# Two small norm tiles in another pool of a two-block fp32 network: the activation pool 160 bytes further on

## The chip, the cores and the metric

One core of a Trainium2 chip runs the whole program. The metric is the device time of one execution in microseconds, as the median of the runs. TensorE multiplies, with a stationary operand (128 x 128, brought in by its own instruction, the weight load) and a moving operand of up to 512 columns; VectorE (DVE), ScalarE (ACT) and GpSimd (POOL) do the rest, and SyncE (SP) issues most DMAs. SBUF, the working memory, has 128 partitions, and a tile takes the same bytes of each; an address below is a byte within a partition.

## What is computed

Two transformer blocks over 512 tokens of width 1024, in fp32. The first block has a mixer (sparse attention beside a matrix memory), a cross attention on a memory of 256 tokens and a feed-forward network; the second has four feed-forward networks, a convolution module and stick-breaking attention. What matters here is that nearly all of the work is matrix products, and that each stage starts with a norm over the features:

```python
def rms_norm(x, gain):
    xf = x.astype(jnp.float32)
    y = xf * lax.rsqrt(jnp.mean(xf * xf, axis=-1, keepdims=True) + NORM_EPS)
    return (y * gain.astype(jnp.float32)).astype(x.dtype)
...
def swiglu_ffn(h, w_gate_up, w_down):
    g, u = jnp.split(h @ w_gate_up, 2, axis=-1)
    return (jax.nn.silu(g) * u) @ w_down
...
def first_block(x, mem, ...):
        h = rms_norm(x, mix_norm_pre[l])
        y = hybrid_mixer(h, ...)
        x = x + rms_norm(y, mix_norm_post[l])
...
        h = rms_norm(x, ffn_norm_pre[l])
        y = swiglu_ffn(h, w_gate_up[l], w_down[l])
        x = x + rms_norm(y, ffn_norm_post[l])
```

## The kernel before

Activations lie feature-major: eight tiles of 128 features x 512 tokens. To keep fp32 accuracy, every operand is split into a rounded part (`hi`, or an `h` at the end of the name) and the remainder (`lo`, or `l`), and a product is three matmuls (`mm3`, lines 169 to 172): weights-hi by x-hi (L170), weights-hi by x-lo (L171), weights-lo by x-hi (L172). In a projection (`proj`, `projs`) the weights are the stationary operand, 128 columns of a slab `whi` or `wlo` at a time, and the activations are the moving operand, 512 columns, or 256 where a stage starts or ends with half of the tokens. In the products that give values token-major (`token_tiles`, L599 on) it is the other way round: 128 columns of `xh` are stationary and 256 columns of weights move. Rows name the output's PSUM tag, then the moving and the stationary operand: `sc<-xh,wlo`.

A feed-forward network (`ffn`) runs two halves. Each half projects 11 feature tiles, gate and up, from `xh` and `xl` (2 x 8 x 3 = 48 matmuls a tile, 528 a half), and multiplies the result, split into `hh` and `hl`, by the down weights (8 x 11 x 3 = 264 matmuls). There are five networks, so ten such halves; in two of the networks the first two feature tiles are projected in halves of the tokens (192 matmuls' worth in all). Other projections from `xh`/`xl` with 512 columns: 17 tiles of the mixer, 5 of the cross attention's queries, 14 of the convolution module, 8 keys and 8 queries of the stick-breaking attention, 24 matmuls each. The convolution module's second projection reads `ch`/`cl`, and half of the mixer's output product reads `yh`/`yl`; all these tiles share the buffers of `xh`/`xl`.

Weights come by DMA from SP's queue into `wraw` (three buffers), and are split by ACT (L126) and DVE (L130) into `whi` and `wlo` (four buffers each). The order of each engine's work is set by a scheduler that goes by data dependencies and a timeline of its own, in some places by hand (`order_pe`, `tick`).

Memory: pools are laid out one behind the other in the order in which they are opened, each tile padded to 32 bytes: `const` (vectors of gains, identity, ones), `act_p` (all activations that live long: `x`, `xh`, `xl`, squares, `rb`, and the small tiles `ms` and `rt` of the norm), `wp` (the weights), and behind these the pools of the stages. `ms` (two buffers of 16 bytes, the mean of squares) and `rt` (three buffers, its inverse root) are written in `rms_sums` (L247 on). From the built program:

| tiles | pool | address of the first | modulo 512 |
|---|---|---|---|
| xh, xl, and ch, cl, yh, yl in their place | act_p | 36,416 | 64 |
| whi, wlo | wp | 93,920 and 110,304 | 224 |
| hh, hl (feed-forward networks) | their own | 134,880 | 224 |
| ynh, ynl (mixer), oh, ol (cross attention) | yn, xp | 126,688 | 224 |
| pTh, and vh, its stationary operand | qp | 204,768 and 200,672 | 480 both |

All of these tiles follow one another at multiples of 1024 bytes, and weights are read in slices of 512 bytes, so that each tile or slice of a row of the table has the same address modulo 512.

Of the kernel before, what the change touches and what calls it, by code (L numbers as in the profile page):

```python
# [9 lines left out]
F32 = mybir.dt.float32  # L10
# [4 lines left out]
P = 128  # L15
S = 512
# [7 lines left out]
NEG = -1.0e30  # L24
# [24 lines left out]
def kernel(ctx: ExitStack, tc: tile.TileContext, t: dict, out: bass.AP):  # L49
# [85 lines left out]
    # heads of 64: the exact product of queries and keys in two passes, (q_hi + q_lo) (k_hi + k_lo), with the  # L135
    # parts of the keys on the two halves of the partitions and each part of the queries on both
# [16 lines left out]
    def head_scores(ps, q, k, i):  # L153
        """scores of query tile i with its keys, the first 128 (i + 1)"""
        n = max((i + 1) * P, 256)
        for c in range(2):
            nc.tensor.matmul(ps[:, :n], q[c][:, i * P : (i + 1) * P], k[:, :n], start=c == 0, stop=c == 1)

    def load_w(ap, width, raw=None, pieces=1, hp=1):
        """a slab of weights as its rounded part and the remainder"""  # L160
        if raw is None:
            raw = wp.tile([P, width], F32, tag="wraw", bufs=3, name=nm("wraw"))
            nc.sync.dma_start(raw, ap)
        hi = wp.tile([P, width], F32R, tag="whi", bufs=4, name=nm("whi"))
        lo = wp.tile([P, width], F32R, tag="wlo", bufs=4, name=nm("wlo"))
        split(raw, hi, lo, pieces=pieces, hp=hp)
        return hi, lo
# [6 lines left out]
    # steps of a latency chain, put between the products of a run that TensorE takes in program order  # L174
# [27 lines left out]
    def square_acc(src, j, state, ts=WHOLE, apart=False, eng=nc.gpsimd):  # L202
        """adds a tile's squares to the running sum; the last tile's may stay apart"""
        if j == KT - 1 and apart:
            if "last" not in state:
                state["last"] = act_p.tile([P, S], F32, tag="sqlast", name=nm("sqlast"))
            nc.scalar.activation(state["last"][:, ts], src[:, ts], AF.Square)
            return
        sq = act_p.tile([P, S], F32, tag="sq", bufs=2, name=nm("sq"))
        nc.scalar.activation(sq[:, ts], src[:, ts], AF.Square)  # L210
        if j == 0:
            state["first"] = sq
        elif j == 1:
            state["acc"] = act_p.tile([P, S], F32, tag="sqacc", name=nm("sqacc"))
            eng.tensor_tensor(state["acc"][:, ts], state["first"][:, ts], sq[:, ts], ALU.add)  # L215
        else:
            eng.tensor_tensor(state["acc"][:, ts], state["acc"][:, ts], sq[:, ts], ALU.add)

    def inv_rms(state, eps=1e-6, ts=WHOLE, psum_only=False):
        """(mean of squares + eps)^-1/2 per token: as a column per token tile, and as a row on all partitions"""  # L220
        if not state:
            for j in range(KT):
                square_acc(x[j], j, state, eng=nc.vector)
        sums = rms_sums(state, eps, ts)
        rt, pb = rms_rows(sums, ts)
        if psum_only:
            return rt, pb
        rb = act_p.tile([P, S], F32, tag="rb", bufs=2, name=nm("rb"))[:, : ts.stop - ts.start]
        nc.vector.tensor_copy(rb, pb)
        return rt, rb  # L230

    def inv_rms_chain(state, first, second):
        """the steps of inv_rms, after that many products each; the result is there when they are done"""
        if not state:
            for j in range(KT):
                square_acc(x[j], j, state, eng=nc.vector)
        got = []

        def finish():
            rt, pb = rms_rows(got[0], WHOLE)  # L240
            rb = act_p.tile([P, S], F32, tag="rb", bufs=2, name=nm("rb"))
            nc.vector.tensor_copy(rb, pb)
            got[:] = [rt, rb]

        chain.append([first, lambda: got.append(rms_sums(state, 1e-6, WHOLE))])
        chain.append([second, finish])
        return got  # L247

    def rms_sums(state, eps, ts):
        n = (ts.stop - ts.start) // P  # L250
        pr = at_tile()
        accs = [state[k] for k in ("acc", "last") if k in state]
        for a, acc in enumerate(accs):
            for i in range(n):
                c = ts.start + i * P
                nc.tensor.matmul(pr[:, 4 * a + i : 4 * a + i + 1], acc[:, c : c + P], ones[:, 0:1], start=True, stop=True)
        ms = act_p.tile([P, 4], F32, tag="ms", bufs=2, name=nm("ms"))
        nc.vector.tensor_scalar(ms[:, :n], pr[:, :n], 1.0 / D, eps, ALU.mult, ALU.add)
        if len(accs) == 2:
            nc.vector.scalar_tensor_tensor(ms[:, :n], pr[:, 4 : 4 + n], 1.0 / D, ms[:, :n], ALU.mult, ALU.add)  # L260
        rt = act_p.tile([P, 4], F32, tag="rt", bufs=3, name=nm("rt"))
        nc.gpsimd.tensor_tensor(rt[:, :n], ms[:, :n], nhalf[:, :n], ALU.pow)
        return rt
# [14 lines left out]
    def post_norm_add(y, state, nxt):  # L278
        """x += y * rb, where y carries its gain already; a step for each half of the tokens"""
# [23 lines left out]
    def ffn(fp, xs, st, wg, wu, wd, out_cb, head=0, tail=0, step=None):  # L303
        """head: F tiles whose projections start with the first half of the tokens; tail: output tiles that end so"""
# [91 lines left out]
    # =====================================================================  # L396
    # hybrid mixer
    # =====================================================================
# [32 lines left out]
    # relative bias: u[h, i] = bias_h(511 - i), masked distances NEG; T[q, c] = -u[127 - q + c]  # L431
# [32 lines left out]
    # gate rows: 0..23 branch gates, 32..35 input gate, 64..67 forget gate  # L464
# [23 lines left out]
    # compressed keys and values  # L488
# [61 lines left out]
    # cumulative gates of the matrix-memory heads  # L550
# [28 lines left out]
    # branch gates, token-major  # L579
# [6 lines left out]
    def token_tiles(chunks, wd, xs_, ntok, cb, ws=None):  # L586
        """out[tokens, wd] for each token tile; chunks hold 1024 / wd K tiles of wd columns"""
# [26 lines left out]
    def coef(sums, h, br, floor):  # L614
        """gate over the sum of the exponentials, per token"""
# [7 lines left out]
    def softmax_rows(ps, bias, ptile, sm, masked):  # L623
        """ps holds the negated scores; writes exp(score - max) to ptile and its row sums to sm"""
# [165 lines left out]
    for hp in range(2):  # L790
# [19 lines left out]
        for i in range(NT):  # L810
# [12 lines left out]
            # num / d, normalized: num * (mean(num^2) + eps d^2)^-1/2 with d = max(|den|, exp(-m))  # L823
# [64 lines left out]
    # =====================================================================  # L888
    # memory cross attention
    # =====================================================================  # L890
# [87 lines left out]
    # P: projection of a feature tile, Q: its query, S, V: a head's scores and values  # L978
# [21 lines left out]
    # =====================================================================  # L1000
    # feed-forward of the first block
    # =====================================================================
# [18 lines left out]
    # =====================================================================  # L1021
    # second block
    # =====================================================================
# [26 lines left out]
    # Depthwise taps on TensorE: 32 channels x 4 taps fill the rows, a diagonal per tap the columns,  # L1050
    # and four such column tiles run side by side; the other taps run on VectorE.
# [45 lines left out]
    def depthwise(j, sets, gl, R, wbd, ts=WHOLE):  # L1097
# [6 lines left out]
        # two independent chains of multiply-adds on VectorE  # L1104
# [17 lines left out]
    def ln_sums(ts):  # L1122
        """mean and variance per token"""
# [31 lines left out]
    def ln_finish(n, lm, m2, ts):  # L1155
        """SiLU of the normalized tiles"""
# [108 lines left out]
    def stick_scores(q, k):  # L1265
        Ws = []
        for i in range(NT):
# [6 lines left out]
            # diagonal block: masked scores  # L1274
# [112 lines left out]
def _tile_cols(w):  # L1387
    """[K, N] -> [N / 128][128 rows of a K tile][K tile][128 columns]"""
    K, N = w.shape
    return np.ascontiguousarray(w.reshape(K // P, P, N // P, P).transpose(2, 1, 0, 3)).reshape(N // P, P, K)  # L1390


def _tile_rows(w, per):
    """[K, N] -> [chunk][128][per K tiles][N]"""
# [4 lines left out]
def _quarters(w):  # L1399
    """groups of 256 columns, each [chunk][128][4 K tiles][256]"""  # L1400
# [112 lines left out]
```

## Time and profile before

| | |
|---|---|
| median of three runs | 2839.34 us (2836.4 to 2841.1) |
| the profiled execution's span, first to last instruction | 2837.0 us |
| TensorE busy in it | 2777.5 us, 98% |
| VectorE, ScalarE, GpSimd busy | 52%, 38%, 12% |
[...]

Of the profiled execution the page gives the span alone; it lies 2.3 us under the median and within the spread of the runs. How to read the views: matmuls overlap, so that the length of one (about 0.39 us) is more than the distance from its start to the next one's, and a busy share near 100% doesn't say how fast TensorE goes. Its pace is read from starts in the order of time, or from counts in a window. A window counts each instruction of which any part lies in it, so that a window of T us that is filled with matmuls of 0.39 us shows (T + 0.39) / pace of them.

### The profile page before, as it was taken

The numbers are of one execution on the slowest core, as the hardware profiler recorded it, in microseconds if no ns is written. First come the engines' busy times: TensorE is split into PE (matmuls) and PEld (weight loads), VectorE is DVE, ScalarE is ACT, GpSimd is POOL, SyncE is SP. The second block draws the span as 40 slices with busy tenths as digits, with TensorE's granted clock in tenths as the row PEclk, the third lists the DMA queues.
The fourth block names the chain that finished last, engine by engine and source line by source line (L and its number), as shares of the span: only waits on it lengthen the run. The fifth ranks groups of instructions, "written<-read, shape, count | busy, mean of one in ns | idle before, by whom it ended". The sixth has DMA issues, their size and how long they took to land.

```text
span 2837.0 us, 35182 instructions
## 1 busy us (share of the span) xinstructions
PE 2777.5 (98%) x13750; PEld 2258.7 (80%) x13750; DVE 1465.4 (52%) x2270; ACT 1075.0 (38%) x1772; POOL 337.9 (12%) x451
## 2 busy tenths in 40 slices
PE   9999999999999999999899999999999997999998
PEld 6877988888888888885688888898888874788887
DVE  7666474643436434449754344434434489543443
ACT  6775544423234222332332233342222366322223
POOL 0133132100002000012210000100000136200001
PEclk9999999999999999999999999999999999999999
DMA  5213321223222232236232322322232310222322
GB/s 199 96 46 105 112 75 58 92 77 109 95 84 90 87 105 96 80 113 171 76 104 86 108 90 83 110 84 101 80 108 87 105 66 3 82 95 84 106 81 81
DMA packets 86923, 263.19 MB, mean 93 GB/s; under 512 B 9655, under 2 KB 13751, under 8 KB 86756
## 3 DMA queue, kind: packets, MB, share of 16 engines
q1 hardware_dynamic: 85148, 258.42, 27.7%
q10 hardware_dynamic: 1608, 2.52, 0.3%
q8 instruction: 108, 1.77, 0.2%
q14 instruction: 59, 0.48, 0.1%
HBM read 256.60 MB, written 4.30 MB: 92 GB/s over the span
## 4 chain that ended last, share of the span: by engine, by line
PE 79%; DVE 4%; DMA 1%; issue 1%; ACT 1%; POOL 0%; SPq 0%; DVEq 0%; ACTq 0%
PE sc L172 9%; PE sc L170 9%; PE sc L171 9%; PE mm L172 7%; PE mm L171 7%; PE mm L170 7%; PE tr L172 6%; PE tr L171 6%; PE tr L170 6%; PE po L172 3%; PE po L170 3%; PE po L171 3%; DVE rm L1280 1%; DVE wlo L130 1%; PE sc L1101 1%
## 5 line engine op out<-in xcount | busy, mean ns | idle before, releaser
L126 ACT ACTIVATE whi<-wraw 128x1024 fp32r<-128x1024 f32 (+3 forms) x518 | 492.2, 955 | 1327.0 <-PE sc L171 458.2
L130 DVE TENSOR_TENSOR wlo<-wraw,whi 128x1024 fp32r<-128x1024 f32 (+4 forms) x559 | 581.6, 1049 | 388.3 <-ACT whi L126 387.4
L170 PE MATMUL mm<-xh,whi 128*128 128x512 f32 (+1 forms) x760 | 291.5, 384 | 5.7 <-ACT whi L126 5.7
L171 PE MATMUL mm<-xl,whi 128*128 128x512 f32 (+1 forms) x760 | 290.5, 382 | 5.5 <-DVE xl L133 5.5
L172 PE MATMUL mm<-xh,wlo 128*128 128x512 f32 (+1 forms) x760 | 291.7, 384 | 0.0
L172 PE MATMUL sc<-xh,wlo 128*128 128x512 f32 (+1 forms) x696 | 274.4, 394 | 0.0
L170 PE MATMUL sc<-xh,whi 128*128 128x512 f32 (+1 forms) x696 | 273.3, 393 | 0.0
L171 PE MATMUL sc<-xl,whi 128*128 128x512 f32 (+1 forms) x696 | 272.6, 392 | 0.0
L171 PE MATMUL tr<-xl,whi 128*128 128x512 f32 (+1 forms) x592 | 226.0, 382 | 2.0 <-DVE xl L133 2.0
L172 PE MATMUL tr<-xh,wlo 128*128 128x512 f32 (+1 forms) x592 | 227.1, 384 | 0.0
L170 PE MATMUL tr<-xh,whi 128*128 128x512 f32 (+1 forms) x592 | 226.2, 382 | 0.0
L215 POOL TENSOR_TENSOR sqacc<-sq,sq 128x512 f32<-128x512 f32 (+1 forms) x11 | 16.4, 1487 | 1618.6 <-issue 915.6
L316 DVE TENSOR_TENSOR su<-sc,rb 128x512 f32<-128x512 f32 x80 | 55.2, 691 | 265.2 <-PE sc L172 265.2
L171 PEld LDWEIGHTS mm<-xl,whi 128*128 128x128 f32 x760 | 144.9, 191 | 35.8 <-DVE xl L133 6.9
L170 PEld LDWEIGHTS mm<-xh,whi 128*128 128x128 f32 x760 | 144.8, 191 | 35.3 <-ACT whi L126 5.7
L172 PEld LDWEIGHTS mm<-xh,wlo 128*128 128x128 f32 x760 | 145.3, 191 | 28.4 <-DVE wlo L130 0.3
L170 PEld LDWEIGHTS sc<-xh,whi 128*128 128x128 f32 x696 | 130.7, 188 | 33.5 <-issue 3.4
L171 PEld LDWEIGHTS sc<-xl,whi 128*128 128x128 f32 x696 | 130.7, 188 | 31.5
L172 PEld LDWEIGHTS sc<-xh,wlo 128*128 128x128 f32 x696 | 130.7, 188 | 30.4
L171 PEld LDWEIGHTS tr<-xl,whi 128*128 128x128 f32 x592 | 112.3, 190 | 26.1 <-DVE xl L133 2.2
L170 PE MATMUL sc<-hh,whi 128*128 128x512 f32 (+1 forms) x352 | 132.6, 377 | 0.0
L171 PE MATMUL sc<-hl,whi 128*128 128x512 f32 (+1 forms) x352 | 132.3, 376 | 0.0
(531 smaller groups left out, 5583.3 us busy)
## 6 DMA issues: line engine op xcount, KB each, us to landing
wraw<-wg SPq DMA_DIRECT2D x110, 512.0 KB, 3.5
wraw<-wu SPq DMA_DIRECT2D x110, 512.0 KB, 3.4
wraw<-wd SPq DMA_DIRECT2D x80, 384.0 KB, 3.0
wraw<-wd SPq DMA_DIRECT2D x80, 320.0 KB, 2.8
wraw<-w_pw SPq DMA_DIRECT2D x24, 512.0 KB, 3.6
wraw<-w_in_f SPq DMA_DIRECT2D x15, 512.0 KB, 4.3
R<-glscr SPq DMA_DIRECT2D x28, 264.0 KB, 5.5
x<-xT SPq DMA_DIRECT2D x16, 256.0 KB, 4.7
```

The costliest lines, as they stand in the source:

```text
L126: last_hi[0] = nc.scalar.activation(hi[:, sl], src[:, sl], AF.Copy)
L130: nc.vector.tensor_tensor(lo[:, sl], src[:, sl], f32(hi[:, sl]), ALU.subtract)
L170: nc.tensor.matmul(ps, lh, rh, start=start, stop=False)
L171: nc.tensor.matmul(ps, lh, rl, start=False, stop=False)
L172: nc.tensor.matmul(ps, ll, rh, start=False, stop=stop)
L215: eng.tensor_tensor(state["acc"][:, ts], state["first"][:, ts], sq[:, ts], ALU.add)
L316: nc.vector.tensor_tensor(su, pu, rb, ALU.mult)
L1101: nc.tensor.matmul(pc[32 * cg : 32 * cg + 32, ts], wbd[:, 4 * g + cg], R[:, cg, 4 * g + ts.start : 4 * g + ts.stop], start=g == 0, stop=g ...
L1280: nc.vector.tensor_tensor_scan(rm[:, :L][:, ::-1], ob[:, 1 : L + 1][:, ::-1], ob[:, 1 : L + 1][:, ::-1], 1.0, ALU.mult, ALU.bypass)
```

## The change

The two small tiles of the norm are allocated in `const` instead of `act_p`:

```diff
@@ rms_sums
-        ms = act_p.tile([P, 4], F32, tag="ms", bufs=2, name=nm("ms"))
+        ms = const.tile([P, 4], F32, tag="ms", bufs=2, name=nm("ms"))
...
-        rt = act_p.tile([P, 4], F32, tag="rt", bufs=3, name=nm("rt"))
+        rt = const.tile([P, 4], F32, tag="rt", bufs=3, name=nm("rt"))
```

Besides, the diff drops comments and docstrings and leaves empty lines in their place. Every engine has the same instructions in the same order as before. Five buffers of 32 bytes make 160: `const` grows by 160 and `act_p` shrinks by as much, so that what lies behind `act_p` stays where it was. In the built program `ms` and `rt` move from 77,376 on to 20,032 on; all tiles of `act_p` ahead of their old place (`x`, `xh`, `xl`, `sq`, `sqacc`, `sqlast`) move up by 160 bytes, `xh`/`xl` to 36,576 on, which is 224 modulo 512; `rb`, the weights and the stages' pools don't move.

## Rows read from the trace of the kernel before

**Rows 1.** The page: span, busy time by engine, TensorE's busy and clock tenths.
```profile
span 2837.0 us, 35182 instructions
PE 2777.5 (98%) x13750; PEld 2258.7 (80%) x13750; DVE 1465.4 (52%) x2270; ACT 1075.0 (38%) x1772; POOL 337.9 (12%) x451
...
PE   9999999999999999999899999999999997999998
...
PEclk9999999999999999999999999999999999999999
```

**Rows 2.** The page: the chain that ended last, shares of the span.
```profile
PE 79%; DVE 4%; DMA 1%; issue 1%; ACT 1%; POOL 0%; SPq 0%; DVEq 0%; ACTq 0%
PE sc L172 9%; PE sc L170 9%; PE sc L171 9%; PE mm L172 7%; PE mm L171 7%; PE mm L170 7%; PE tr L172 6%; PE tr L171 6%; PE tr L170 6%; PE po L172 3%; PE po L170 3%; PE po L171 3%; DVE rm L1280 1%; DVE wlo L130 1%; PE sc L1101 1%
```

**Rows 3.** Busy time by window, projections of feed-forward networks; (x) counts instructions touching it.
```profile
core 0: us, PE busy (x) PEld busy (x) DVE busy (x) ACT busy (x) POOL busy (x), PEclk, DMA share, GB/s
532.00:623.00 91.00, 91.00 (x392) 73.21 (x391) 45.33 (x58) 28.74 (x37) 0.00 (x0) 1.00 0.27 87
684.00:806.00 122.00, 122.00 (x524) 98.16 (x523) 52.57 (x63) 35.09 (x44) 0.00 (x0) 1.00 0.27 91
1063.00:1185.00 122.00, 122.00 (x524) 98.15 (x523) 52.72 (x64) 34.30 (x43) 0.00 (x0) 1.00 0.27 90
1626.00:1748.00 122.00, 122.00 (x524) 98.13 (x523) 53.25 (x64) 34.84 (x43) 0.00 (x0) 1.00 0.27 91
2641.00:2763.00 122.00, 122.00 (x524) 98.14 (x524) 53.05 (x64) 34.63 (x43) 0.00 (x0) 1.00 0.27 91
```

**Rows 4.** The same view, output products of two of these networks.
```profile
624.00:683.00 59.00, 59.00 (x262) 48.84 (x261) 16.98 (x19) 17.17 (x24) 0.00 (x0) 1.00 0.34 106
1186.00:1245.00 59.00, 59.00 (x262) 48.84 (x261) 26.23 (x33) 22.19 (x31) 8.26 (x6) 1.00 0.34 106
```

**Rows 5.** PE matmuls by line, tiles and shape: count | busy us, mean ns | idle before.
```profile
L172 PE MATMUL sc<-xh,wlo 128*128 128x512 f32 x680 | 269.9, 397 | 0.0
L170 PE MATMUL sc<-xh,whi 128*128 128x512 f32 x680 | 268.6, 395 | 0.0
L171 PE MATMUL sc<-xl,whi 128*128 128x512 f32 x680 | 268.1, 394 | 0.0
L171 PE MATMUL sc<-hl,whi 128*128 128x512 f32 x308 | 119.9, 389 | 0.0
L172 PE MATMUL tr<-ch,wlo 128*128 128x512 f32 x8 | 3.2, 399 | 0.0
L172 PE MATMUL tr<-oh,wlo 128*128 128x512 f32 x8 | 3.1, 389 | 0.0
L172 PE MATMUL po<-pTh,vl 128*128 128x512 f32 x2 | 0.8, 389 | 0.0
```

**Rows 6.** PE in order of time, the mixer's output product: start us, length us.
```profile
318.55 0.39 PE L170 MATMUL sc<-ynh,whi 128*128 128x512 f32 x1
...
319.23 0.40 PE L170 MATMUL sc<-yh,whi 128*128 128x512 f32 x1
319.47 0.40 PE L171 MATMUL sc<-yl,whi 128*128 128x512 f32 x1
...
321.35 0.39 PE L170 MATMUL sc<-yh,whi 128*128 128x512 f32 x1
...
322.05 0.40 PE L170 MATMUL mm<-ynh,whi 128*128 128x512 f32 x1
```

**Rows 7.** Products 256 columns wide: PE in order of time, same product, later.
```profile
350.43 0.28 PE L170 MATMUL mm<-ynh,whi 128*128 128x256 f32 x1
...
351.39 0.28 PE L172 MATMUL mm<-ynh,wlo 128*128 128x256 f32 x1
```

**Rows 8.** Busy time by window: shared values, convolution, stick-breaking attention.
```profile
1875.00:1900.00 25.00, 25.00 (x213) 25.00 (x212) 5.82 (x6) 9.85 (x16) 0.00 (x0) 1.00 0.25 85
1246.00:1441.00 195.00, 183.63 (x1129) 134.45 (x1129) 150.29 (x240) 60.49 (x95) 49.52 (x41) 0.96 0.44 123
2268.00:2475.00 207.00, 188.95 (x901) 134.53 (x900) 161.62 (x233) 116.98 (x240) 90.48 (x138) 0.98 0.15 51
```

**Rows 9.** PE's waits: us in total, times, longest.
```profile
PE sc L1101 <- DMA R<-glscr: 5.3, 2, 3.3
PE sc L157 <- ACT be L1278: 4.9, 7, 1.5
```

**Rows 10.** The instruction that writes the small tile rt: count | busy us, mean ns | idle before.
```profile
L262 POOL TENSOR_TENSOR rt<-ms,nhalf 128x4 f32<-128x4 f32 x10 | 13.9, 1386 | 176.8 <-DVE ms L258 149.9 <-DVE ms L260 26.8
```

## The prediction

> **What bounds the kernel now.** Begin with the page: TensorE is busy for 98% of a span of 2837.0 us, and its clock is granted in full in nearly every slice [rows 1]. The chain that ended last agrees: 79% of the span are TensorE's, and the lines named are the three matmuls of a split product, L170 to L172, whatever the PSUM tag [rows 2]. VectorE's waits and all DMA together are a few per cent. So the time is the number of matmuls times their pace, and whoever wants to move it has to change one of these two. The change has the same instructions in the same order; what is left is the pace, and the reader should next ask whether it is the same everywhere.
>
> It isn't. Take the windows that are filled with projections of the feed-forward networks: 524 matmuls touch 122 us in each of four of them, and 392 touch 91 us in a fifth, at full clock [rows 3]. With (T + 0.39) / count that is (579 + 1.95) / 2488 = 233.5 ns from start to start. The windows filled with these networks' output products show 262 in 59 us, so 59.39 / 262 = 226.7 ns, also at full clock [rows 4]. Both kinds have 512 columns, 128 x 128 weights out of the same buffers, the same triple of matmuls; TensorE doesn't idle in either. The other engines can't be the cause: DVE is busy for 52.57 of 122 us in the slow kind, and DMA's share is smaller there (0.27 against 0.34), not larger [rows 3, 4]. What differs is the tile that moves: `xh`/`xl` (64 modulo 512) in the slow kind, `hh`/`hl` (224, as the weights) in the fast one.
>
> The lengths of single matmuls say the same by tile. With `xh`/`xl` they are 397, 395 and 394 ns in the three lines, with `hl` 389 [rows 5]. `ch`, in `xh`'s buffers but in another stage and by another producer, takes 399 on L172, `oh`, at 224, takes 389 on the same line and in the same function, and `pTh` with `vh`, both at 480, take 389 too [rows 5]. So it is neither the stage nor the function; nor is it the weights' region, since `vh` doesn't lie there.
>
> Cleanest is the mixer's output product, where one accumulation takes `ynh`/`ynl` (224) for four K tiles and then `yh`/`yl` (64) for four, against the same slab. Three steps from 318.55 to 319.23 make 227 ns a matmul; nine from 319.23 to 321.35 make 236 [rows 6]. Nothing else changes at 319.23. After the change back at 322.05 the pace needs some products to recover, so it depends on how the streams stand to each other and not only on the single instruction; in a long run of one kind it is steady.
>
> **The change part by part.** *Removed and added:* nothing on any engine. The 19 small instructions that write `ms` and `rt` (POOL's take 1386 ns for four columns [rows 10]) take the same operands from another address. I cost this at nothing: no row shows an instruction of this kind at two addresses, so the bounds are an assumption, a tenth of its length either way for all 19, that is 19 x 0.14 = 2.6 us; most of them run while TensorE has other products to do, and I take the middle.
>
> *Moved:* all tiles of `act_p` that TensorE reads, from 64 to 224 modulo 512. That makes the moving operand equal to the weights modulo 512, as `hh` and `oh` are today. I take their pace for it. First term, the feed-forward networks: ten halves of 528 matmuls less the 192 that run on half of the tokens are 5,088. At 233.5 - 226.7 = 6.8 ns each that is 34.6 us. All of it is on the path, since TensorE doesn't wait in these windows.
>
> Second term, the other 512-column matmuls out of `act_p`: 52 projections (17 mixer, 5 cross attention, 14 convolution, 8 and 8 keys and queries) of 24 are 1,248, and `ch` (96) and `yh` (60) make 1,404. At the same 6.8 ns (the lengths in rows 5 differ by 5 to 10 ns, so 7 to 14 us are the bounds) that is 9.5 us. Not all of it can be kept. In the convolution module TensorE waits for `R` to come back from memory (5.3 us [rows 9]; busy for 183.63 of 195 us [rows 8]), and in the stick-breaking attention for ACT and DVE (188.95 of 207 us [rows 8]; 4.9 us of it for `be` [rows 9]); what it gains ahead of such a wait it waits longer. These are 336 and 192 matmuls, 3.6 us. I take off half, 1.8 us; the ends are nothing and 3.6.
>
> Third term, the 256-column matmuls with an operand in `act_p`, some 1,944 (624 of `xh` on half of the tokens, 672 where weights move over a stationary `xh`, 384 of the memory tokens, 192 of `ch`, 72 of `yh`). The shared values, with unequal addresses, run at 25.28 / 213 = 118.7 ns [rows 8]. Equal addresses give 0.96 / 8 = 120.0 ns in `ynh`'s halves [rows 7]. So here the change costs, at most 1.3 x 1,944 = 2.5 us; at least nothing. I take 1.3 us.
>
> *What else reads the moved tiles:* DVE, ACT and POOL split, square and add them. These engines are busy for 52%, 38% and 12% of the span [rows 1], and in the slow windows DVE has more than half of the time free [rows 3], which hides any change of some nanoseconds. The cover holds after the change too: a slab of weights is then used up in 24 x 226.7 ns = 5.4 us instead of 5.6, and in the output products the supply keeps up at that pace with a higher DMA share [rows 4].
>
> *Sum:* 34.6 + 9.5 - 1.8 - 1.3 = 41.0 us. The profiled span of 2837.0 would go to 2796. The median of the runs lies 2.3 us higher and goes to 2839.3 - 41.0 = 2798.3, say **2798**. The ends of the terms: 34.6 + 14 = 48.6 at best, 34.6 + 7 - 3.6 - 2.5 = 35.5 at worst, or 2791 and 2804.
>
> **The rivals.** *The pool, not the offset.* Every slow tile lies in `act_p`, every fast one outside; no row shows a tile of `act_p` at the weights' offset. If the pace goes by the region of memory (some higher bit of the address, or who else works there), the change doesn't do what it says, and the time stays: 2839, or 2842 with the third term in full. Against it: the fast tiles lie in three regions, `hh` from 134,880, `oh` from 126,688, `pTh` from 204,768, and share only the equality modulo 512; and `ch`, `yh` and `xh` are slow with three different producers. I give it 9%.
> [...]
>
> *The gain is paid back outside the networks.* TensorE comes earlier to every wait of the mixer, the convolution and the attentions, and the stages end when they ended before. Then only the first term is left, less the third: 2839.3 - 34.6 + 2.5 = 2807. For it: the waits of rows 9 and the stages of rows 8. Against it: even there TensorE is busy over 90% of the time. 10%.
>
> *Slower: equal is not the best offset for all of the streams.* In the networks' projections two products follow each other out of different slabs, and after the change a weight load and a moving read could meet in a way that the output products don't have. The place is the same 6,492 matmuls; the worst step that a row shows with an `act_p` tile is near 0.24 us (319.23 to 319.47 [rows 6]), 6 ns over today's mean. That gives 2839.3 + 6,492 x 0.006 = 2878. It decides as soon as the mean pace exceeds today's by 5.7 us / 6,492 = 0.9 ns. Against it: the output products have the same triple, slices and buffers, and stand at 226.7 in both windows read [rows 4]. 3%.
>
> **How the numbers follow.** The forecast gets the remaining 78%, with 2791 to 2804 from the ends of its terms, and 2 to 3 us to each side for the spread of the runs. The range reaches to the paid-back case, too: **2791 to 2810**, which leaves out the first and the third rival and some of the tails, near 2 in 10. A measurement of this kernel can tell 0.2%, 5.7 us, from no change. The forecast and the paid-back case are both faster: 0.88; same is the first rival, 0.09; slower the third, 0.03.
>
> **What would show it.** In the profile after, the windows of the networks' projections show as many matmuls per microsecond as those of the output products: 122 us hold 540 (122.39 / 0.2267), not 524. The lengths with `xh`, `ch` and `yh` fall to 389. In the mixer's output product the pace no longer changes between `ynh` and `yh`. The window of shared values goes from 118.7 to about 120 ns. The waits for `R` and `be` grow by a microsecond or two in total. If the first rival holds, none of the lengths change; if the second does, they do, and the waits grow by some 8 us. I am wrong if lengths fall and the time doesn't follow, or if `xh` lands between 389 and 395, which would mean that more than the offset is at work.

## Result, and the profile after

| | before | after |
|---|---|---|
| median of the runs | 2839.77 us (4 runs, 2836.4 to 2841.1) | 2802.59 us (4 runs, 2799.86 to 2802.88) |
| ratio, with its 95% interval | | 0.9867 [0.9853, 0.9881] |
| span of the profiled execution | 2837.0 us | 2801.1 us |
| TensorE busy, idle in that span | 2777.5, 59.5 us | 2737.0, 64.1 us |

Faster by 37.2 us where 41.0 were forecast: 2802.6 instead of 2798, within the range of 2791 to 2810. The interval of the ratio allows a gain of 33.8 to 41.7 us, so the times alone don't tell the two apart; what came out otherwise has to be read from the profiles. The page has the first sign of what came out otherwise:

```profile
span 2801.1 us, 35182 instructions
PE 2737.0 (98%) x13750; PEld 2257.9 (81%) x13750; DVE 1465.4 (52%) x2270; ACT 1074.2 (38%) x1772; POOL 338.2 (12%) x451
```

Against [rows 1], TensorE's busy time fell by 40.5 us, the span only by 35.9: the idle time grew by 4.6. No other engine's busy time moved by a microsecond.

Busy time by window, after: the first five windows are projections of the networks and answer to [rows 3], the next two their output products ([rows 4]), the last the shared values ([rows 8]).

```profile
core 0: us, PE busy (x) PEld busy (x) DVE busy (x) ACT busy (x) POOL busy (x), PEclk, DMA share, GB/s
532.00:620.00 88.00, 88.00 (x390) 72.85 (x389) 45.45 (x58) 28.70 (x37) 0.00 (x0) 1.00 0.28 89
681.50:800.00 118.50, 118.50 (x524) 98.13 (x523) 52.59 (x63) 35.02 (x44) 0.00 (x0) 1.00 0.29 94
1053.50:1172.00 118.50, 118.50 (x524) 98.12 (x523) 52.98 (x64) 34.48 (x43) 0.00 (x0) 1.00 0.29 94
1608.00:1726.00 118.00, 118.00 (x523) 97.69 (x522) 52.93 (x64) 34.44 (x43) 0.00 (x0) 1.00 0.29 94
2608.50:2727.00 118.50, 118.50 (x524) 98.15 (x523) 53.02 (x64) 34.51 (x43) 0.00 (x0) 1.00 0.29 94
621.50:680.00 58.50, 58.50 (x260) 48.44 (x259) 17.03 (x19) 17.22 (x24) 0.00 (x0) 1.00 0.36 107
1173.00:1231.00 58.00, 58.00 (x258) 48.02 (x257) 25.98 (x33) 22.40 (x31) 8.28 (x6) 1.00 0.36 108
...
1850.00:1875.00 25.00, 25.00 (x211) 25.00 (x210) 4.90 (x4) 7.80 (x12) 0.00 (x0) 1.00 0.26 85
```

The same 524 matmuls that touched 122 us now touch 118.5. With the forecast's formula the five windows give (561.5 + 5 x 0.39) / 2485 = 226.7 ns, where [rows 3] gave 233.5; the output products stay at (116.5 + 0.78) / 518 = 226.4 by the window and 226.7 from their starts. The shared values go the other way, from 118.7 to 25.28 / 211 = 119.8 ns.

Lengths by line, tiles and shape, after, against [rows 5]:

```profile
L170 PE MATMUL sc<-xh,whi 128*128 128x512 f32 x680 | 265.4, 390 | 0.0
L171 PE MATMUL sc<-xl,whi 128*128 128x512 f32 x680 | 264.7, 389 | 0.0
L172 PE MATMUL sc<-xh,wlo 128*128 128x512 f32 x680 | 264.6, 389 | 0.0
...
L172 PE MATMUL tr<-ch,wlo 128*128 128x512 f32 x8 | 3.1, 389 | 0.0
```

`xh`, `xl` and `ch` have come to 389 to 390 ns. In the mixer's output product, where the pace changed from 227 to 236 ns in the middle of an accumulation [rows 6], it doesn't change any more (start and length in us):

```profile
316.87 0.39 PE L170 MATMUL sc<-ynh,whi 128*128 128x512 f32 x1
...
318.23 0.39 PE L170 MATMUL sc<-yh,whi 128*128 128x512 f32 x1
...
320.95 0.39 PE L170 MATMUL mm<-ynh,whi 128*128 128x512 f32 x1
```

Six steps of `ynh`/`ynl` take 1.36 us and twelve of `yh`/`yl` 2.72: 226.7 ns in both.

TensorE's waits, after (us in total, times, longest), against [rows 9]:

```profile
PE sc L269 <- POOL rt L262: 7.4, 4, 2.7
PE sc L1101 <- DMA R<-glscr: 6.9, 3, 2.8
...
PE sc L157 <- ACT be L1278: 5.1, 7, 1.5
...
PE po L269 <- POOL rt L262: 1.3, 1, 1.3
```

The waits for `R` and `be` that the forecast named grew by 1.6 and 0.2 us (of the 1.6, 1.0 stood under `gl` L1080, whose data `R` carries, in the profile of before). The one that grew most is another, for `rt`, the norm's inverse root. Before it was:

```profile
PE sc L269 <- POOL rt L262: 5.1, 4, 2.0
```

So 5.1 became 7.4 + 1.3 us in this pair of profiles. Other profiles, further on, show that the faster pace isn't what made this wait grow.

### The profile page after: what moved, and what is told of

Same layout as the page of the kernel before. It is cut to its first block, busy times and chain, and to the rows that moved or that the text cites. A ratio compares the mean times of both kernels' runs of the same rounds, so it can differ in the third digit from the quotient of the medians.

```text
span 2801.1 us, 35182 instructions
## 1 busy us (share of the span) xinstructions
PE 2737.0 (98%) x13750; PEld 2257.9 (81%) x13750; DVE 1465.4 (52%) x2270; ACT 1074.2 (38%) x1772; POOL 338.2 (12%) x451
## 4 chain that ended last, share of the span: by engine, by line
PE 79%; DVE 4%; issue 1%; ACT 1%; DMA 1%; SPq 0%; POOL 0%; DVEq 0%; ACTq 0%
PE sc L170 9%; PE sc L171 9%; PE sc L172 9%; PE mm L171 7%; PE mm L170 7%; PE mm L172 7%; PE tr L170 6%; PE tr L171 6%; PE tr L172 6%; PE po L170 3%; PE po L171 3%; PE po L172 3%; DVE c L1113 1%; DVE wlo L130 1%; PE po L1310 1%
## 5 line engine op out<-in xcount | busy, mean ns | idle before, releaser
L170 PE MATMUL mm<-xh,whi 128*128 128x512 f32 (+1 forms) x760 | 287.8, 379 | 5.8 <-ACT whi L126 5.8
L171 PE MATMUL mm<-xl,whi 128*128 128x512 f32 (+1 forms) x760 | 287.0, 378 | 5.5 <-DVE xl L133 5.5
L172 PE MATMUL mm<-xh,wlo 128*128 128x512 f32 (+1 forms) x760 | 286.8, 377 | 0.0
L170 PE MATMUL sc<-xh,whi 128*128 128x512 f32 (+1 forms) x696 | 270.1, 388 | 0.0
L171 PE MATMUL sc<-xl,whi 128*128 128x512 f32 (+1 forms) x696 | 269.2, 387 | 0.0
L172 PE MATMUL sc<-xh,wlo 128*128 128x512 f32 (+1 forms) x696 | 269.1, 387 | 0.0
L171 PE MATMUL tr<-xl,whi 128*128 128x512 f32 (+1 forms) x592 | 223.2, 377 | 1.9 <-DVE xl L133 1.9
L170 PE MATMUL tr<-xh,whi 128*128 128x512 f32 (+1 forms) x592 | 223.6, 378 | 0.0
L172 PE MATMUL tr<-xh,wlo 128*128 128x512 f32 (+1 forms) x592 | 223.5, 378 | 0.0
L215 POOL TENSOR_TENSOR sqacc<-sq,sq 128x512 f32<-128x512 f32 (+1 forms) x11 | 16.3, 1485 | 1585.4 <-issue 896.0
L170 PEld LDWEIGHTS mm<-xh,whi 128*128 128x128 f32 x760 | 145.0, 191 | 31.9 <-ACT whi L126 5.8
L171 PEld LDWEIGHTS mm<-xl,whi 128*128 128x128 f32 x760 | 144.9, 191 | 31.5 <-DVE xl L133 7.0
L172 PEld LDWEIGHTS mm<-xh,wlo 128*128 128x128 f32 x760 | 144.8, 191 | 25.1 <-DVE wlo L130 0.3
L170 PEld LDWEIGHTS sc<-xh,whi 128*128 128x128 f32 x696 | 130.7, 188 | 29.6 <-issue 2.5
L172 PEld LDWEIGHTS sc<-xh,wlo 128*128 128x128 f32 x696 | 130.7, 188 | 26.7
L171 PEld LDWEIGHTS sc<-xl,whi 128*128 128x128 f32 x696 | 130.7, 188 | 26.1
L170 PE MATMUL sc<-hh,whi 128*128 128x512 f32 (+1 forms) x352 | 132.6, 377 | 0.0
L171 PE MATMUL sc<-hl,whi 128*128 128x512 f32 (+1 forms) x352 | 132.2, 376 | 0.0
L172 PE MATMUL sc<-hh,wlo 128*128 128x512 f32 (+1 forms) x352 | 132.2, 376 | 0.0
```

What stands on the lines that cost most here:

```text
L170: nc.tensor.matmul(ps, lh, rh, start=start, stop=False)
L171: nc.tensor.matmul(ps, lh, rl, start=False, stop=False)
L172: nc.tensor.matmul(ps, ll, rh, start=False, stop=stop)
```

## Experiments: is it the difference of the addresses?

**The small tiles and the absolute place.** The theory is that the pace goes by how the moving tiles lie against the weights. The rivals are that the new place of `ms` and `rt` does it, or the new address of the activations by itself. The changed kernel gets a pad of the 160 bytes that it had freed, so that the activations keep their new address (224 modulo 512) and all that lies behind goes 160 bytes further too: the difference is the old one again.

```diff
 def rms_sums(state, eps, ts):
+    if not padded:
+        padded.append(act_p.tile([P, 40], F32, name="pad"))
     ms = const.tile([P, 4], F32, tag="ms", bufs=2, name=nm("ms"))
```

> The small tiles ms and rt lie in const as in the changed kernel, but 160 bytes of padding stand at their old place in act_p. So act_p lies at 224 modulo 512 as in the changed kernel, and the weights and all that follows go on to 384: the moving xh/xl stand to the weights as before (160 bytes apart), hh and oh are equal to them. Theory (the difference between moving operand and weights decides): xh/xl stay at 233.4 ns from start to start, lengths 394 to 397, and the time is that of the kernel before, 2839 +- 4. Rival (the place of ms and rt, or the absolute offset 224 of act_p, decides): 226.7 ns, lengths 389, and 2803. If the 4.6 us of new idle time come with the place of ms and rt, 2844.

Measured: 2838.56 us (10 runs) against 2838.76 for the kernel before, ratio 0.9999 [0.9989, 1.0009].

```profile
L172 PE MATMUL sc<-xh,wlo 128*128 128x512 f32 x680 | 270.0, 397 | 0.0
...
L171 PE MATMUL sc<-hl,whi 128*128 128x512 f32 x308 | 119.9, 389 | 0.0
```

These are the lengths of [rows 5] to the nanosecond, with the small tiles in `const` and the activations at the address that they have in the changed kernel. Neither place matters by itself. Nor does new idle time come with the small tiles' place: TensorE idles for 60.4 us here, for 59.5 before. `rt`'s instruction takes 1386 ns for four columns as before [rows 10].

**The other way round.** From the kernel before: the weights' pool is opened ahead of the activations'. Weights and `xh` then both lie at 64 modulo 512, and `hh`, which was fast, lies 160 bytes off the weights.

```diff
-    act_p = ctx.enter_context(tc.tile_pool(name="act_p", bufs=1))
     wp = ctx.enter_context(tc.tile_pool(name="wp", bufs=3))
+    act_p = ctx.enter_context(tc.tile_pool(name="act_p", bufs=1))
```

> The kernel before, with the pool of the weights opened ahead of act_p; ms and rt stay in act_p. Weights and xh/xl are then both at 64 modulo 512, in other regions of memory than before (weights from 32,320, xh from 81,472), and hh, ynh, oh, sh stay at 224, now 160 bytes off the weights. Theory (difference modulo 512): xh/xl fall to 226.7 ns and length 389; hh/hl rise from 226.7, to 233.4 if +160 costs what -160 did. With 2,508 matmuls of hh and some 370 of oh, sh and ynh at 6.7 ns slower, 19 us over the changed kernel: 2822, bounds 2803 (no cost at +160) to 2838 (238 ns). Rival (the region or pool of the tile decides): xh/xl stay at 233.4, hh at 226.7, 2839.

Measured: 2821.17 us (4 runs), ratio 0.9936 [0.9921, 0.9951].

```profile
L170 PE MATMUL sc<-xh,whi 128*128 128x512 f32 x680 | 265.4, 390 | 0.0
...
L172 PE MATMUL sc<-hh,wlo 128*128 128x512 f32 x308 | 122.2, 397 | 0.0
```

The two kinds have changed places: `xh` runs at 226.7 ns and `hh` at 234.3. No tile is slow because of its pool, its stage or who writes it. This kernel has the fast pace in the 5,088 matmuls of the projections and loses it in the 2,508 output products of 512 columns, so its gain is about half.

**Which differences?** In the changed kernel a pad ahead of the networks' own pools puts `hh` and `hl` off the weights, by another number of bytes in each of the five networks; nothing else that streams moves. Three kernels try 15 differences. The edit of the first of them, in which `idx` counts the networks and the first network has a line of its own:

```diff
     fp = fs.enter_context(tc.tile_pool(name="fp", bufs=1))
+    fp.tile([P, 8], F32, name="pad0")
...
         with tc.tile_pool(name=f"fp{idx}", bufs=1) as fp:
+            if [32, 64, 128, 192, 256][idx]:
+                fp.tile([P, [32, 64, 128, 192, 256][idx] // 4], F32, name=f"pad{idx}")
```

> The changed kernel, with 32, 64, 128, 192 and 256 bytes of padding ahead of the tiles of the five feed-forward networks, so that hh/hl stand that far from the weights modulo 512 in the first to the fifth. It measures the pace of the output products by difference. Theory: xh/xl stay at 226.7 ns in all; hh/hl differ by network, and none is faster than 226.7; each within 226.7 to 238. Time 2803 to 2803 + 2,508 x 11 ns = 2831. Rival (the region decides, or only one difference is bad): all five at 226.7, 2803.

> As the run before, with 320, 384, 448, 160 and 352 bytes. 352 is what xh/xl had in the kernel before (64 - 224 = -160), so the fifth network's output products, in another region and out of other tiles, should show 233.4 ns with the slow L172 (238 against 231) if the difference modulo 512 is the cause, and 226.7 if xh's place was. The fourth, at 160, is what hh has when the weights are moved ahead of act_p. Time 2803 to 2831.

> The changed kernel with 288, 416, 480, 224 and 96 bytes ahead of the tiles of the five networks. The two scans before gave 226.7 ns at 0 and 256, 229.0 at 64 and 320, 233.3 at 32, 128, 192, 384 and 448, 234.3 at 160, 233.4 at 352, so the pace seems to repeat every 256 bytes. Theory (the difference modulo 256): 288 as 32, 233.3; 416 as 160, 234.3; 96 as 352, 233.4 with one matmul of three at 238; 480 and 224 equal to each other, at an unknown pace between 226.7 and 238. Rival (modulo 512, and 256 a lucky other value): 288, 416 and 96 come out otherwise, or 480 and 224 differ. Time 2803 plus 2,508 x 6.6 ns, 2820 +- 4.

Measured, one run each: 2811.67, 2815.84 and 2819.77 us. Busy time by window: output products at differences of 32, 64 and 256 in the first of these kernels, of 160 in the second, of 416 in the third. All windows are 58 us long, so that fewer matmuls (x) mean a slower pace.

```profile
620.50:678.50 58.00, 58.00 (x250) 46.59 (x249) 15.40 (x18) 16.36 (x24) 0.00 (x0) 1.00 0.35 105
995.30:1053.30 58.00, 58.00 (x255) 47.59 (x254) 20.27 (x26) 13.41 (x17) 0.00 (x0) 1.00 0.35 108
2557.50:2615.50 58.00, 58.00 (x258) 48.02 (x257) 20.86 (x26) 13.57 (x17) 0.00 (x0) 1.00 0.35 108
```
```profile
2006.30:2064.30 58.00, 58.00 (x250) 46.61 (x249) 19.85 (x25) 12.74 (x17) 0.00 (x0) 1.00 0.34 103
```
```profile
997.00:1055.00 58.00, 58.00 (x249) 46.60 (x249) 19.49 (x25) 12.84 (x16) 0.00 (x0) 1.00 0.35 105
```

Taken finer, as the mean distance of starts over the 264 output matmuls of a half (in the three networks in which both halves have 264 of 512 columns, the two agree to 0.1 ns):

| moving minus weights, bytes modulo 512 | ns from start to start |
|---|---|
| 0 (after) and 256 | 226.7, 226.7 |
| 64 and 320 | 229.0, 229.0 |
| 32, 288; 128, 384; 192, 448; 224, 480 | 233.3 in all eight |
| 96 and 352 | 233.4, 233.4 |
| 160 and 416 | 234.3, 234.3 |

Every difference tried has the pace of the one 256 bytes away: the period in these kernels is 256, not 512. Equality is the fastest of the differences tried, and nothing lies below 226.7. The old place of `xh`, 64 - 224 = -160, is 96 modulo 256, and 233.4 ns is what it ran at; [rows 3] gave 233.5. At 96 and 352, too, one step of three takes 238 ns and two take 231.

**256 apart, in full.** The changed kernel with 256 bytes between the activations and the weights:

```diff
+    pad_b = ctx.enter_context(tc.tile_pool(name="pad_b", bufs=1))
+    pad_b.tile([P, 64], F32, name="pad1")
     wp = ctx.enter_context(tc.tile_pool(name="wp", bufs=3))
```

> The changed kernel with 256 bytes of padding between act_p and the weights, so that weights, hh and oh lie at 480 and xh/xl at 224 modulo 512: 256 apart, equal modulo 256. Theory (modulo 256): xh/xl at 226.7 ns, length 389, time 2803 +- 3, as the changed kernel. Rival (the equality modulo 512 is needed, as the change's words say): 233.4 ns, 2839.

Measured: 2800.58 us (4 runs), ratio to the kernel before 0.9863 [0.9846, 0.9879], the changed kernel's within the interval. The projections' window holds as many as after the change:

```profile
679.00:797.00 118.00, 118.00 (x523) 97.70 (x521) 52.58 (x63) 34.67 (x44) 0.00 (x0) 1.00 0.29 93
```

## Experiments: which weights, and does it linger?

In a triple (whi by xh, whi by xl, wlo by xh) the weights of the next matmul are loaded while one runs. In the kernel before, a load (PEld) starts with the matmul ahead of its own and is over in 0.19 us, that matmul in 0.40:

```profile
683.79 0.40 PE L171 MATMUL tr<-xl,whi 128*128 128x512 f32 x1
683.79 0.19 PEld L172 LDWEIGHTS tr<-xh,wlo 128*128 128x128 f32 x1
684.02 0.40 PE L172 MATMUL tr<-xh,wlo 128*128 128x512 f32 x1
684.02 0.19 PEld L170 LDWEIGHTS tr<-xh,whi 128*128 128x128 f32 x1
```

Two kernels part the triple.

**The low weights 128 bytes off the high ones** (a pad between `whi` and `wlo`, another behind so that what follows keeps its difference to `whi`):

```diff
     hi = wp.tile([P, width], F32R, tag="whi", bufs=4, name=nm("whi"))
+    if not padded:
+        padded.append(wp.tile([P, 32], F32, bufs=1, name="pad0"))
     lo = wp.tile([P, width], F32R, tag="wlo", bufs=4, name=nm("wlo"))
```

> The changed kernel with the weights' remainders wlo 128 bytes further on than whi, and the stages' pools 256 further, so that moving operands stand at 0 (modulo 256) to whi and at 128 to wlo everywhere. In the row of three matmuls, L170 moves while whi is loaded for L171, L171 moves while wlo is loaded for L172, L172 moves while whi is loaded for the next L170. Theory A (the moving read meets the load of the weights that come next): only L171 gets slower, to some 233 to 246 ns, the others stay near 227. Theory B (the moving operand's own weights count): only L172 gets slower. Theory C (the streams stay out of step for long): all three. With a third of some 9,400 matmuls at 6.6 ns: 2803 + 21 = 2824, bounds 2811 and 2843.

Measured: 2833.8 us (one run). PE in order of time, a projection of this kernel; its lines 176 to 178 are L170 to L172 of the others:

```profile
699.91 0.39 PE L176 MATMUL sc<-xh,whi 128*128 128x512 f32 x1
700.13 0.40 PE L177 MATMUL sc<-xl,whi 128*128 128x512 f32 x1
700.37 0.40 PE L178 MATMUL sc<-xh,wlo 128*128 128x512 f32 x1
700.60 0.39 PE L176 MATMUL sc<-xh,whi 128*128 128x512 f32 x1
```

Mean steps to the next start are 226.7, 232.5 and 234.2 ns in all twenty runs of matmuls (ten of projections, ten of output products). None of the three theories on record has this: two of the three are slow. The one (L177, 232.5 ns) streams while the far weights are being loaded for its successor. The other (L178, 234.2 ns) multiplies with the far weights while near ones are being loaded, but it is also the one right behind a slowed matmul; which of the two slows it, this kernel doesn't separate.

**The low inputs 128 bytes off** (the tiles `xl`, with `cl` and `yl` in their buffers, which stream against `whi` in the middle product):

```diff
+    pad_b.tile([P, 32], F32, name="pad1")
     wp = ctx.enter_context(tc.tile_pool(name="wp", bufs=3))
...
     xa, x = load_x()
+    for j in range(KT):
+        act_p.tile([P, S], F32R, tag=f"xh{j}", name=f"hold_h{j}")
+    act_p.tile([P, 32], F32, name="pad0")
+    for j in range(KT):
+        act_p.tile([P, S], F32R, tag=f"xl{j}", name=f"hold_l{j}")
```

> The changed kernel with one thing apart: the low halves of the inputs (every tile xl, and they alone) lie 128 bytes off their place, so that in the split products whi by xh, whi by xl and wlo by xh only the middle one reads at another offset modulo 256 than its own weights; the order of the instructions is the changed kernel's. Theory N (a matmul is slowed only where the inputs it streams stand apart, modulo 256 bytes, from weights that are loaded beside it, and nothing lingers): only the middle product of the networks' projections goes from 226.7 to about 233 ns, the other two stay at 226.7; a third of the 4,822 projection matmuls by 6.6 ns, 10.6 us, so some 2813 us. Theory L (the slowing lingers into the matmul that follows): the middle and the last product slow, about 21 us, 2824 us. Rival: all three slow, 2834 us. The networks' products with the hidden values stay at 226.7 in all of them.

Measured: 2816.37 us (one run), between the two theories. PE in order of time in the second half of the first network, where lines 177 to 179 are L170 to L172:

```profile
700.32 0.39 PE L177 MATMUL sc<-xh,whi 128*128 128x512 f32 x1
700.54 0.40 PE L178 MATMUL sc<-xl,whi 128*128 128x512 f32 x1
700.78 0.39 PE L179 MATMUL sc<-xh,wlo 128*128 128x512 f32 x1
701.00 0.39 PE L177 MATMUL sc<-xh,whi 128*128 128x512 f32 x1
```

Here it is as theory N has it: steps of 226.7, 234.1 and 225.9 ns, 228.9 in the mean. That holds in all five second halves and in the first half of the fourth network. The other four first halves start at 233.3 ns, at the same differences. In the second network the mean falls to 231 behind the 15th triple and to 228.9 from the 25th on; in the first and the fifth it falls to 231.1 within ten triples and stays there to the end; in the third it stays at 233.3:

```profile
1500.66 0.40 PE L177 MATMUL tr<-xh,whi 128*128 128x512 f32 x1
1500.89 0.40 PE L178 MATMUL tr<-xl,whi 128*128 128x512 f32 x1
1501.13 0.39 PE L179 MATMUL tr<-xh,wlo 128*128 128x512 f32 x1
1501.36 0.40 PE L177 MATMUL tr<-xh,whi 128*128 128x512 f32 x1
```

The rhythm that a half ends with has lasted for 75 us or more. The second halves follow without a break on a steady run of output products. Every first half is broken near its start by small matmuls of the norm (`ident` by `rt`), and it is behind these that it takes up one rhythm or another. In the fourth network, the only one to run at 228.9 at once, the break stands ahead of the middle product, in the others ahead of the first of a triple; whether that is the reason wasn't tried. So where only a part of the triple is out of step, the addresses don't settle the pace alone: something of the start lasts. Why one start gives one rhythm and not another stays open. In the kernels with one difference for all three (before, after, and those of the table) every half of a kind ran at one pace, but in the kernel before the start shows as well: the long step of 238 ns falls on L170 in the first halves of the first, third and fifth networks, on L171 in the fourth's, and on L172 in the second's and in all second halves. It is not tied to one of the three products.

## Why the prediction was right, and which of its terms was too large

**The pace by place: right.** The step "What differs is the tile that moves" held, and the first rival fell twice over: the activations' new address at the old difference gains nothing (0.9999), and the pool opened elsewhere changes the pace with the difference. In this kernel, at a granted clock of 1.00 and with TensorE never idle in these windows, 233.3 against 226.7 ns hang on how the moving tile's address stands to the weights'. The forecast said "modulo 512", since that was what the table of addresses showed; 256 is enough, and no step of the sum depends on it.

**First term: right.** The five networks, each from the projection behind the norm's small matmuls (`ident` by `rt`) to its last output product (in two networks the last one ahead of the next norm's small matmuls), took 1713.0 us in all and take 1680.5, by the starts in the two traces: 32.5 us. Of the 5,088 matmuls 4,822 lie in these stretches; the other 266, at 6.7 ns, are an estimate of 1.8 us ahead of them. Together 34.3, forecast 34.6.

**Second term: the step that was mis-sized.** All that lies outside these stretches was to gain 9.5 - 1.8 - 1.3 = 6.4 us. It went from 1124.0 to 1120.6; less the 1.8 of the first term's, 1.6 are left. By stage, in us:

| stage | before | after | gain |
|---|---|---|---|
| mixer and cross attention (to the first network) | 531.4 | 531.6 | -0.2 |
| first to second network | 47.2 | 46.7 | 0.5 |
| convolution module | 215.5 | 213.0 | 2.5 |
| keys and values | 104.6 | 103.7 | 0.9 |
| stick-breaking attention | 206.6 | 206.7 | -0.1 |
| tail | 18.6 | 18.9 | -0.3 |

The forecast took losses off the convolution and the stick-breaking attention alone. What wasn't in the sum is that the mixer and the cross attention, with 588 of the 1,404 matmuls or 3.9 us, keep next to nothing.

How firm is this? A stage's length varies by itself from profile to profile, so all of them are needed: two with `xh` at the slow pace (before, and the pad of 160 bytes), five with `xh` fast and all else of these stages as after (after, the three kernels of the table, 256 apart). "Weights ahead" stays out, since `oh` and `ynh` are slow in it. In us:

| stage | slow | fast |
|---|---|---|
| mixer and cross attention | 531.4, 530.2 | 531.6, 530.2, 530.9, 531.7, 528.7 |
| convolution module | 215.5, 213.4 | 213.0, 212.6, 211.5, 213.3, 212.0 |
| keys and values | 104.6, 104.6 | 103.7 in all five |
| stick-breaking attention | 206.6, 206.9 | 206.7, 206.1, 205.9, 206.1, 205.9 |
| all outside the networks | 1124.0, 1121.3 | 1120.6, 1118.2, 1118.4, 1120.4, 1116.0 |

The gain of the keys and values is clear, 0.9 us. The convolution's 2.5 us of the first pair is not: the pad's kernel has 213.4 at the slow pace. The means differ by 0.2 us in the mixer and cross attention, and single profiles by up to 3; that most of the counted 3.9 us is absent there is what they show. In all, the means differ by 3.9 us; less the 1.8 of the first term's, 2.1 of the forecast 6.4 are left.

Busy time by window, this stage before and after:

```profile
10.00:531.40 521.40, 510.77 (x3105) 432.34 (x3105) 329.84 (x751) 302.92 (x658) 124.54 (x192) 0.98 0.28 94
```
```profile
10.00:531.60 521.60, 506.51 (x3108) 430.75 (x3107) 330.10 (x751) 303.19 (x659) 124.48 (x192) 0.99 0.29 94
```

TensorE's busy time falls by 4.3 us and its idle time grows from 10.6 to 15.1, by 4.5: in this pair of profiles nearly all of the 4.6 that the span lost to the busy time. Not all of it is the change's work. With the pad, at the slow pace, TensorE idles for 13.1 us in this stage; in the five fast profiles for 13.0 to 16.3.

Where a gain goes shows at the mixer's end, in the wait for `rt`. The POOL instruction that writes it starts at 356.16 and again at 371.37 us before, at 354.57 and 369.81 after, at 356.24 and 371.47 with the pad, at 355.62 and 370.86 with 256 apart. That is 15.2 us from one to the next in these four, and in the other six profiles too: the work of VectorE and POOL up to `rt` doesn't go faster with TensorE's products, and what they gain within it is lost. How it is lost differs. Before, the granted clock is down to half (0.50 from 366 to 370 us) behind a wait for `xl`; PE's starts with their idle time, then windows:

```profile
364.89 0.39 PE L171 MATMUL mm<-xl,whi 128*128 128x256 f32 x1 [1.96 <-DVE xl L133]
```
```profile
366.00:370.00 4.00, 4.00 (x20) 4.00 (x20) 4.00 (x7) 1.93 (x4) 3.56 (x4) 0.50 0.37 117
370.00:374.00 4.00, 4.00 (x26) 4.00 (x26) 2.43 (x9) 0.11 (x1) 1.38 (x2) 0.69 0.35 126
```

After, TensorE comes 1.6 us earlier, waits as long, and keeps its clock; but then it is too early for `rt`, and the lower clock falls on what follows:

```profile
363.30 0.39 PE L171 MATMUL mm<-xl,whi 128*128 128x256 f32 x1 [1.94 <-DVE xl L133]
370.57 0.43 PE L269 MATMUL sc<-ident,rt 128*128 128x128 f32 x2 [2.66 <-POOL rt L262]
```
```profile
366.00:370.00 4.00, 1.91 (x16) 1.71 (x15) 3.70 (x8) 1.02 (x2) 2.19 (x3) 1.00 0.40 127
370.00:374.00 4.00, 3.43 (x22) 3.43 (x23) 2.46 (x7) 1.69 (x4) 2.98 (x5) 0.75 0.06 23
```

Matmul by matmul, the kernel after leads by 1.6 us at 365 (0.5 of it since the first 33 us), by 4.4 at 372 and by 0.3 from 376 on; at 395, behind the next `rt` and another stretch of lower clock (from 390 to 394 us 0.63 before and 0.50 after), the lead is -1.2.

Which of the two ways it goes isn't set by the pace. With the pad, at the slow pace, TensorE waits 2.65 us for `rt` at 372.24, with its clock at 1.00 from 364 to 372. "Weights ahead" and the second kernel of the table, at the fast pace, have the lower clock there (0.61 and 0.57 from 364 to 372) and wait for 0.2 us or less. PE's waits for `rt` in the mixer and cross attention, in the order before, after, pad, 256 apart:

```profile
PE sc L269 <- POOL rt L262: 2.7, 2, 1.7
```
```profile
PE sc L269 <- POOL rt L262: 5.4, 3, 2.7
```
```profile
PE sc L273 <- POOL rt L266: 5.4, 3, 2.6
```
```profile
PE sc L271 <- POOL rt L264: 5.4, 3, 2.7
```

In the whole span these waits are 7.7 us with the pad and 7.6 with 256 apart. So their growth between the two profiles of the section on the result isn't a sign of the faster pace, and why the clock falls here in some executions and not in others stays open. What is shown is that the way from one `rt` to the next keeps its 15.2 us at either pace. The forecast read the waits for `R` and `be` and left out `rt`, which stood beside them with 5.1 us.

The second rival's mechanism, then, holds for a part of the second term: with the third term's cost of 0.7 us, some 2.8 of its 7.7 are left and some 5 are gone. Its time of 2807 lies outside the interval, which reaches to 2806.0.

**Third term: right in kind.** The shared values went from 118.7 to 119.8 ns, forecast 120.0. The cost was laid on 1,944 matmuls of 256 columns. Those with `xh` moving stay near 119.8 ns from start to start in both kernels, so that it falls on the 672 with `xh` stationary: 0.7 us, forecast 1.3.

**Small tiles: right,** nothing, and the bound of 2.6 us was wide: the kernel with these tiles alone differs by 0.2 us. The forecast counted 19 instructions that write `ms` and `rt`; 19 write `rt`, and 28 more on VectorE write `ms`.

**The third rival** fell: no offset among the sixteen is better than equality for 512 columns, and the projections with two slabs run at the output products' pace.

## What to carry to other kernels

When TensorE is busy throughout, compare its pace from stage to stage by starts in order of time; a busy share near 100% hid a difference of 3% here. Where two stages of the same shape differ, compare the addresses of the moving tile and of the weights: here 256-byte equality was worth 32.5 us in the five networks, for a change that moves no instruction, and any edit that adds or drops a few small tiles ahead of such a pool can win or lose it unnoticed. Count the gain only where TensorE is the last to be ready: list every wait of the stages around, the short ones on norms too, and expect the lead to be gone at the first of them (at the mixer's end a lead of 4.4 us at 372 was 0.3 at 376, behind the wait for `rt`). And read a wait in several executions before putting its growth down to a change: here one pair of profiles showed a growth that other profiles of the old pace had as well.

## What the runs showed of the hardware

- In these kernels the pace of 512-column fp32 matmuls with 128 x 128 weights went by the difference of the moving tile's address and the weights', modulo 256 bytes, where all three products had the same one: 226.7 ns at equality, 229.0 at 64, 233.3 to 234.3 elsewhere in steps of 32.
- With `wlo` alone 128 bytes off, the steps are 226.7, 232.5 and 234.2 ns: the second matmul runs while the far weights are loaded for the third. The third has its own weights out of step and follows a slowed one; which of the two counts isn't shown.
- With `xl` alone 128 bytes off, the same addresses ran at 228.9, 231.1 or 233.3 ns, each to the end of a half and for 75 us or more. What chooses among them wasn't found.
- Products of 256 columns had it otherwise: the networks' last output tiles ran at 116.7 ns a matmul at differences of 32 and 288, at 117.4 at 160, at 117.8 at 320, and at 119.9 at equality, but also at 96 and 352. Why wasn't tried.
- At the mixer's end, from one `rt` to the next, the kernel took 15.2 us in all ten profiles, at either pace of TensorE. The granted clock from 364 to 372 us was 1.00 in six of them and 0.57 to 0.61 in four, at either pace.
